# Output stage of a hybrid decoder layer: the subtractions that make the low parts of the feed-forward operands are queued behind the next tile's norm

## The chip, the cores and the metric

The kernel runs on one core of a Trainium2 chip. The core has TensorE (PE: products and transposes, results into PSUM), VectorE (DVE), ScalarE (ACT), GpSimd (POOL, which reads and writes SBUF here) and a queue, SyncE (SP), that issues all loads and stores. Each engine takes its own instructions in order; between engines there are semaphores. The metric is device time of one execution in microseconds, lower is better; several runs give a median.

## What is computed

One layer of a decoder with 1024 tokens, plus 16 meta tokens, and width 1024:

```python
u = rmsnorm(h, attn_norm_w[l]); proj = u @ w_in[l]
o_gdn = gated_deltanet_group(...)
o_fox = forgetting_attention_group(...)
h = h + concatenate([o_gdn, o_fox], -1) @ w_out[l]
x = rmsnorm(h, ffn_norm_w[l])
h = h + (silu(x @ w_gate) * (x @ w_up)) @ w_down
return rmsnorm(h, final_norm_w)[:, 16:]
```

The change touches what lies between the third last and the second last line of the layer: the residual sum after the output projection, the norm, and the preparation of `x` for the feed-forward products.

## The kernel before

All large products take operands that are split in two: a high part (ScalarE casts the value to the matmul type) and a low part (value minus high part), and three products high x high, high x low, low x high are summed. So every operand needs a cast on ScalarE and a subtraction on VectorE or GpSimd.

The output stage works on eight tiles of 128 tokens, in the order 0, 4, 1, 5, 2, 6, 3, 7 (`ORDER`). Tile t and tile t + 4 belong together: the feed-forward products follow a Strassen-like scheme with seven products p1 to p7 over 2 x 2 blocks, and the sums of its left operands are made from such a pair of tiles. For each tile the stage does this:

1. `prep_load`: a load of the attention output `of` (512 KB) is issued on SP; GpSimd sums its two halves (L1133); ScalarE spreads the softmax reciprocals `rinv` into the half that came free (L1134).
2. `prep_pe`: TensorE transposes that half (`rbt`, L1144), VectorE multiplies (L1145), ScalarE casts and VectorE subtracts (`split`, L161 and L162), which gives `ohl`.
3. `load_h` loads the residual `hst`, whose slot is that of the tile two before.
4. `out_fox(tt, 0)` and `out_fox(tt, 1)`: twelve products each (`wof`, `wx`) for the left and the right half of the columns; VectorE adds each to `hst` (L1177). In six of the tiles (4, 5, 2, 6, 3, 7) the second half has twelve further products ahead of it, `fox_g`, for the DeltaNet group.
5. `norm2`, behind the second half: ScalarE squares and sums (L1067), VectorE makes the mean (L206), GpSimd takes the power -1/2 (L207), VectorE scales (L1069); the result is `xn2`, in the trace `xn`. A store of `hst` follows.
6. `u_blocks`: TensorE transposes `xn2` into two PSUM banks (`u2t`, L1248; three banks take turns). In tiles 0 to 3 the inner function `put` makes p1 and p2, each a cast (L1253) and a low part (L1254, VectorE), and ScalarE copies both banks into `br` (L1261) for the partner tile. In tiles 4 to 7 VectorE forms the differences (L1267 to L1271, GpSimd one at L1273) and `put` makes p6, p3, p7 with VectorE and p5, p4 with GpSimd (`ul_p` are the low parts, `uh_p` the high ones).

`u_blocks` of a tile stands in the program between two halves of the next tile, so that its transposes run among the next tile's products: the transposes of tile 1, for instance, follow twelve products of tile 5. TensorE's order is the one of the program (`manual_schedule`). The orders of the other engines come from a scheduler that places each instruction by a timeline of its own when the program is built; `tc.issue_after(x)` adds that an instruction is placed behind x.

With tile 7 the first products of the feed-forward begin (`ga`, `ua`, then `gb`, L1343). Ahead of them VectorE and ScalarE split the weights (`wlo_g`, `wlo_u`, and from L1317 on the sums `ws`, `s4` and their splits); the latter stand behind tile 7's second residual sum (`last_h`).

## Time and profile before

| what | value |
|---|---|
| median of 3 runs | 1329.59 us (1329.17 to 1331.01) |
| profiled execution | 1326.59 us |
| its span | 1324.9 us |
| TensorE busy | 1294.3 us (98%) |
| VectorE, ScalarE, GpSimd busy | 853.2, 548.4, 440.6 us |
| output stage | about 605 to 700 us of the span |

The span is what the instructions cover; the execution has 1.7 us around it. The profiled execution is one run, 3.0 us below the median of the three. A row of an engine's timeline has the start, the duration, the line, what it writes and reads (numbers left out), and in brackets how long the engine had been idle and what ended that. A duration holds the instruction's start-up and its end, so rows that follow each other without a gap overlap by some 0.1 us (VectorE, ScalarE) or 0.15 us (TensorE).

### The profile page before, as it was taken

How to read it: one execution, taken by the hardware profiler on the slowest of the kernel's cores; microseconds unless marked ns; L12 is line 12 of the kernel's file. 1: busy time of each engine (PE TensorE's matmuls, PEld its weight loads, DVE VectorE, ACT ScalarE, POOL GpSimd, SP SyncE). 2: the span in 40 equal slices, each digit the busy share in tenths (PEclk: the TensorE clock that was granted, in tenths of full speed). 3: DMA queues.
4: the chain of work that ended last, by engine and by line, in shares of the span. 5: the costliest groups of instructions: out<-in, count | busy, mean ns of one | idle time of the engine just before them, and what ended most of it. 6: DMA issues, size and time to landing. Idle time of an engine off the chain costs nothing.

```text
span 1324.9 us, 20216 instructions
## 1 busy us (share of the span) xinstructions
PE 1294.3 (98%) x7442; PEld 1129.3 (85%) x7442; DVE 853.2 (64%) x1521; ACT 548.4 (41%) x918; POOL 440.6 (33%) x415
## 2 busy tenths in 40 slices
PE   8999999999999999999999999999999999999997
PEld 8999999899999877887777888888888888888886
DVE  6665889676236578896787665566666565355644
ACT  6543534232223477884553233333333343343332
POOL 2211323501022266661522644553334453010301
PEclk9999999999999999999999999999999999999999
DMA  6331743874479698746544555444444557945513
GB/s 227 98 112 33 212 133 116 221 209 143 150 246 329 195 271 233 206 114 199 182 144 130 188 183 183 147 140 159 159 162 156 175 193 271 400 176 189 210 62 128
DMA packets 192955, 237.93 MB, mean 180 GB/s; under 512 B 18896, under 2 KB 144712, under 8 KB 189144
## 3 DMA queue, kind: packets, MB, share of 16 engines
q1 hardware_dynamic: 192856, 236.65, 55.8%
q8 instruction: 58, 0.95, 0.3%
q14 instruction: 41, 0.34, 0.1%
HBM read 159.00 MB, written 77.60 MB: 179 GB/s over the span
## 4 chain that ended last, share of the span: by engine, by line
PE 76%; DVE 8%; DMA 7%; issue 3%; POOL 3%; ACT 1%; SPq 1%; POOLq 0%; DVEq 0%; ACTq 0%
PE xp L1506 8%; PE yp L1506 7%; PE gb L1343 5%; PE ud L1343 5%; PE ub L1343 5%; PE gd L1343 5%; PE ua L1343 4%; PE ga L1343 4%; PE pj_fk L201 4%; PE pj_fq L201 3%; PE ue L1343 2%; PE ge L1343 2%; PE pt L989 2%; PE fv L201 2%; DMA rkr<-rk_d 1%
## 5 line engine op out<-in xcount | busy, mean ns | idle before, releaser
L162 DVE TENSOR_TENSOR al_p<-ra_p,ah_p 128x2048 fp32r<-128x2048 f32 (+1 forms) x21 | 46.7, 2222 | 93.9 <-ACT ah_p L161 93.9
L942 POOL TENSOR_TENSOR bi<-ccol,cr 128x144 f32<-128x144 f32 (+7 forms) x60 | 70.6, 1182 | 50.8 <-DVE sm L958 35.6
L161 ACT CAST ah_p<-ra_p 128x2048 fp32r<-128x2048 f32 (+1 forms) x21 | 37.1, 1767 | 105.7 <-PE xp L1506 48.5
L1506 PE MATMUL xp<-wh_p,ah_p 128*128 128x512 f32 (+1 forms) x187 | 70.5, 377 | 0.7 <-DVE hs L1533 0.7
L1506 PE MATMUL xp<-wl_p,ah_p 128*128 128x512 f32 (+1 forms) x187 | 70.4, 377 | 0.0
L1506 PE MATMUL xp<-wh_p,al_p 128*128 128x512 f32 (+1 forms) x187 | 70.4, 376 | 0.0
L1396 POOL TENSOR_TENSOR gzw<-gzw,uzt 128x512 f32<-128x512 f32 x11 | 18.4, 1676 | 154.4 <-DVE uzt L1387 128.5
L1396 POOL TENSOR_TENSOR gxy<-gxy,uxy 128x512 f32<-128x512 f32 x22 | 38.9, 1769 | 66.6 <-DVE uxy L1387 57.4
L1343 PE MATMUL gb<-uh_p,w_g_p 128*128 128x512 f32 x176 | 57.8, 389 | 0.0
L1343 PE MATMUL gd<-uh_p,w_g_p 128*128 128x512 f32 x176 | 57.7, 389 | 0.0
L1343 PE MATMUL ud<-uh_p,w_u_p 128*128 128x512 f32 x176 | 57.7, 389 | 0.0
L1343 PE MATMUL ub<-uh_p,w_u_p 128*128 128x512 f32 x176 | 57.7, 389 | 0.0
L162 DVE TENSOR_TENSOR w_u_p<-raw_u,w_u_p 128x512 fp32r<-128x512 f32 x42 | 42.7, 1016 | 21.6 <-ACT w_u_p L161 21.5
L162 DVE TENSOR_TENSOR pl<-pt,ph 128x512 fp32r<-128x512 f32 (+1 forms) x96 | 51.8, 553 | 5.0 <-ACT ph L161 4.4
L161 ACT CAST ph<-pt 128x512 fp32r<-128x512 f32 (+1 forms) x96 | 45.2, 473 | 21.2 <-PE pt L989 20.5
L963 ACT ACTIVATE pr<-pr,sm 128x144 f32<-128x144 f32 (+3 forms) x64 | 50.6, 790 | 7.8 <-DVE sm L958 6.8
L1343 PE MATMUL ga<-uh_p,w_g_p 128*128 128x512 f32 x160 | 52.5, 389 | 0.0
L1343 PE MATMUL ua<-uh_p,w_u_p 128*128 128x512 f32 x160 | 52.5, 389 | 0.0
L1506 PE MATMUL yp<-wh_p,ah_p 128*128 128x512 f32 x132 | 51.3, 389 | 0.0
L1506 PE MATMUL yp<-wl_p,ah_p 128*128 128x512 f32 x132 | 51.3, 389 | 0.0
L1506 PE MATMUL yp<-wh_p,al_p 128*128 128x512 f32 x132 | 51.3, 389 | 0.0
L162 DVE TENSOR_TENSOR wl_p<-rw_p,wh_p 128x2048 fp32r<-128x2048 f32 (+1 forms) x21 | 46.9, 2235 | 3.4 <-ACT wh_p L161 3.4
(630 smaller groups left out, 4291.4 us busy)
## 6 DMA issues: line engine op xcount, KB each, us to landing
ra_p<-ao_p SPq DMA_DIRECT2D x14, 1024.0 KB, 4.7
raw_g<-in_w_gate_dram SPq DMA_DIRECT2D x22, 512.0 KB, 4.9
raw_u<-in_w_up_dram SPq DMA_DIRECT2D x22, 512.0 KB, 5.4
raw_d<-in_w_down_dram SPq DMA_DIRECT2D x22, 512.0 KB, 7.1
wt_p<-raw_d SPq DMA_DIRECT2D x33, 256.0 KB, 2.3
rw_p<-wt_p SPq DMA_DIRECT2D x8, 1024.0 KB, 5.7
kk<-k_d SPq DMA_DIRECT2D x14, 520.0 KB
rw_p<-in_w_down_dram SPq DMA_DIRECT2D x6, 1024.0 KB
```

Source lines behind the costliest of these rows:

```text
L161: cast = nc.scalar.copy(dst_hi, src)
L162: tail[0] = (cast, nc.vector.tensor_sub(dst_lo, src, dst_hi.bitcast(F32)))
L201: nc.tensor.matmul(dst, a, b, start=first, stop=last)
L942: nc.gpsimd.tensor_tensor(bi[:, :n], ccol[:, h, j:j + 1].broadcast_to([P, n]), cr[:, :n], op=ALU.subtract)
L963: nc.scalar.activation(pr[:, :n], pr[:, :n], AF.Exp, bias=sm[:, np_ - 1:np_], scale=-1.0, accum_out=rsum[:, h, j:j + 1])
L989: nc.tensor.transpose(pt[:rows_k, P * j:P * j + P], pts[j][0][:, c0:c0 + rows_k], ident)
L1343: nc.tensor.matmul(dst, a[:, c], b[:, k], start=(first and k == 0 and i == 0), stop=(k == 3 and i == 2), skip_group_check=not first)
L1396: last_mul[0] = G.tensor_tensor(gs[d], gs[d], us[d], op=ALU.mult)
L1506: nc.tensor.matmul(dst[:, n_], a[:, f, c], b[:, f, n_], start=(first and i == 0 and n == 0), stop=(i == NF - 1 and n == 2), skip_group_che ...
```

## The change

`norm2` returns its two last instructions, the power and the scaling. `put` no longer issues the low part, but keeps it in a list, `late`; the function `u_late` issues the list, each placed behind the power and the scaling of the tile whose norm was built last. `u_late` runs after the second half of the next tile. For the tiles 0, 4, 1, 5, 2 and 6 the low parts thus come behind the norm of 4, 1, 5, 2, 6 and 3. For the tiles 3 and 7 (`defer` false) the low part follows its cast as before. Casts, copies and differences are issued where they were.

```diff
--- before.py
+++ after.py
@@ -1065,8 +1065,8 @@
     def norm2(src, wb, dst, pool, nm):
         sst = pool.tile([P, 4], F32, tag="st2", bufs=2, name=f"st2_{nm}")
         nc.scalar.activation(dst, src, AF.Square, accum_out=sst[:, 0:1])
-        inv_rms(sst[:, 2:3], sst[:, 0:1], 1, 1.0 / D, sst[:, 1:2])
-        V.scalar_tensor_tensor(dst, src, sst[:, 2:3], wb, op0=ALU.mult, op1=ALU.mult)
+        pw = inv_rms(sst[:, 2:3], sst[:, 0:1], 1, 1.0 / D, sst[:, 1:2])
+        return pw, V.scalar_tensor_tensor(dst, src, sst[:, 2:3], wb, op0=ALU.mult, op1=ALU.mult)
 
     def wout_w(k0, nb):
         return w_out[P * k0:P * k0 + 256, 512 * nb:512 * nb + 512].rearrange("(k p) n -> p k n", p=P)
@@ -1156,7 +1156,7 @@
             nc.sync.dma_start(ht, h_d[tt])
         pre_u[tt] += (ht,)
 
-    accs, last_h = {}, [None]
+    accs, last_h, norms, late = {}, [None], [], []
 
     def fox_g(tt):
         if tt in fused:
@@ -1177,7 +1177,7 @@
         last_h[0] = V.tensor_add(hb, acc, hb)
         if nb:
             xn = wo_tile("xn2", [P, D], 2, tt)
-            norm2(ht, nwb2, xn, wo2, f"f{tt}")
+            norms[:] = norm2(ht, nwb2, xn, wo2, f"f{tt}")
             nc.sync.dma_start(h_d[tt], ht)
             xns[tt] = xn
 
@@ -1238,7 +1238,12 @@
         uo[p] = og["h"][i], og["l"][i]
     tops = {}
 
-    def u_blocks(tt):
+    def u_late():
+        with tc.issue_after(norms[0].ins), tc.issue_after(norms[1].ins):
+            while late:
+                late.pop(0)()
+
+    def u_blocks(tt, defer=True):
         xn, cols = xns[tt], slice(P * (tt % 4), P * (tt % 4) + P)
         pts = []
         for g in range(2):
@@ -1251,7 +1256,9 @@
         def put(p, src, eng=None):
             hi, lo = (t[:, :, cols] for t in uo[p])
             nc.scalar.copy(hi, src)
-            (eng or V).tensor_tensor(lo, src, hi.bitcast(F32), op=ALU.subtract)
+            late.append(lambda: (eng or V).tensor_tensor(lo, src, hi.bitcast(F32), op=ALU.subtract))
+            if not defer:
+                late.pop()()
 
         if tt < 4:
             br2 = wo_tile("br", [P, 2, 4, P], 1, tt, slot="br")
@@ -1429,10 +1436,11 @@
                     prep_load(ORDER[i + 2])
             if i > 2:
                 fox_g(tt)
-                u_blocks(ORDER[i - 1])
+                u_blocks(ORDER[i - 1], i < NT - 1)
             out_fox(tt, 1)
             if i < 3:
                 u_blocks(ORDER[i - 1])
+            u_late()
             if i == 2:
                 for m, v in (("g", w_g_v), ("u", w_u_v)):
                     raw0[m] = wraw.tile([P, WMAX], F32, tag="raw", name=f"raw_{m}")[:, :D]
@@ -1452,7 +1460,7 @@
         with tc.issue_after(last_h[0].ins):
             for m in "gu":
                 next(gens[m])
-        u_blocks(ORDER[7])
+        u_blocks(ORDER[7], False)
         for j in range(NF):
             ffn_in(j, () if j else done, None if j else gens)
             down_sums(j)
```

TensorE has the same instructions in the same order as before. VectorE, ScalarE, GpSimd and the load queue have the same instructions in another order. Three places follow, the second on two engines; a name such as `ohl_5_7713` is the tile `ohl` of token tile 5 and a buffer number.

ScalarE, tiles 0 and 4, from the cast of p1 to the square of tile 1's norm (`xn2_1`). Before:

```order
L1253 CAST uh_p1_7625<-u2t_0_0_7682 128x4x128
L1067 ACTIVATE xn2_4_7675,st2_f4_7676<-hst_4_7556 128x1024
L1253 CAST uh_p2_7629<-u2t_0_1_7687 128x4x128
L1261 COPY br_0_7692<-u2t_0_0_7682 128x512
L1261 COPY br_0_7692<-u2t_0_1_7687 128x512
L161 CAST ohl_5_7713<-of_5_7580 128x512
L1134 COPY of_2_7725<-rinv_96 128x512
L1067 ACTIVATE xn2_1_7743,st2_f1_7744<-hst_1_7660 128x1024
```

The same stretch of ScalarE's queue now:

```order
L1258 CAST uh_p1_7625<-u2t_0_0_7682 128x4x128
L1268 COPY br_0_7692<-u2t_0_0_7682 128x512
L1067 ACTIVATE xn2_4_7675,st2_f4_7676<-hst_4_7556 128x1024
L1258 CAST uh_p2_7629<-u2t_0_1_7687 128x4x128
L1268 COPY br_0_7692<-u2t_0_1_7687 128x512
L1134 COPY of_2_7725<-rinv_96 128x512
L161 CAST ohl_5_7713<-of_5_7580 128x512
L1067 ACTIVATE xn2_1_7743,st2_f1_7744<-hst_1_7660 128x1024
```

The first copy into `br_0` has moved ahead of the square of tile 4, and the spreading of `rinv` for tile 2 (`of_2`) ahead of the cast of tile 5's attention output (`ohl_5`).

ScalarE, tiles 4 and 1, from the last cast of tile 4 to the square of tile 5's norm. Before:

```order
L1253 CAST uh_p4_4146<-br_0_7692 128x4x128
L1134 COPY of_6_7807<-rinv_96 128x512
L161 CAST ohl_2_7795<-of_2_7725 128x512
L1442 ACT_TABLE_LOAD
L1442 ACTIVATE sil_7861<-mhalf_94 128x1
L1253 CAST uh_p1_7625<-u2t_1_0_7824 128x4x128
L1253 CAST uh_p2_7629<-u2t_1_1_7829 128x4x128
L1261 COPY br_1_7834<-u2t_1_0_7824 128x512
L1261 COPY br_1_7834<-u2t_1_1_7829 128x512
L1067 ACTIVATE xn2_5_7854,st2_f5_7855<-hst_5_7722 128x1024
```

The same stretch of ScalarE's queue now:

```order
L1258 CAST uh_p4_4146<-br_0_7692 128x4x128
L1134 COPY of_6_7807<-rinv_96 128x512
L1258 CAST uh_p1_7625<-u2t_1_0_7824 128x4x128
L1268 COPY br_1_7834<-u2t_1_0_7824 128x512
L1258 CAST uh_p2_7629<-u2t_1_1_7829 128x4x128
L1268 COPY br_1_7834<-u2t_1_1_7829 128x512
L161 CAST ohl_2_7795<-of_2_7725 128x512
L1450 ACT_TABLE_LOAD
L1450 ACTIVATE sil_7861<-mhalf_94 128x1
L1067 ACTIVATE xn2_5_7852,st2_f5_7853<-hst_5_7722 128x1024
```

The cast of tile 2's attention output (`ohl_2`) has moved behind the two casts and two copies that read tile 1's transposes, and each copy follows its cast.

GpSimd, tiles 4 to 2, from the power of tile 1's norm (`st2_f1`) to that of tile 2's. Before:

```order
L207 TENSOR_TENSOR st2_f1_7744<-st2_f1_7744,mhalf_94 128x1
L1133 TENSOR_TENSOR of_6_7807<-of_6_7807 128x512
L1254 TENSOR_TENSOR ul_p5_4147<-br_0_7692,uh_p5_4145 128x4x128
L1254 TENSOR_TENSOR ul_p4_4148<-br_0_7692,uh_p4_4146 128x4x128
L1133 TENSOR_TENSOR of_3_7889<-of_3_7889 128x512
L207 TENSOR_TENSOR st2_f5_7855<-st2_f5_7855,mhalf_94 128x1
L1273 TENSOR_TENSOR br_1_7834<-br_1_7834,ub_5_7916 128x512
L1254 TENSOR_TENSOR ul_p5_4147<-br_1_7834,uh_p5_4145 128x4x128
L1133 TENSOR_TENSOR of_7_7979<-of_7_7979 128x512
L1254 TENSOR_TENSOR ul_p4_4148<-br_1_7834,uh_p4_4146 128x4x128
L207 TENSOR_TENSOR st2_f2_7947<-st2_f2_7947,mhalf_94 128x1
```

The same stretch of GpSimd's queue now:

```order
L207 TENSOR_TENSOR st2_f1_7744<-st2_f1_7744,mhalf_94 128x1
L1259 TENSOR_TENSOR ul_p5_4147<-br_0_7692,uh_p5_4145 128x4x128
L1133 TENSOR_TENSOR of_6_7807<-of_6_7807 128x512
L1259 TENSOR_TENSOR ul_p4_4148<-br_0_7692,uh_p4_4146 128x4x128
L207 TENSOR_TENSOR st2_f5_7853<-st2_f5_7853,mhalf_94 128x1
L1133 TENSOR_TENSOR of_3_7889<-of_3_7889 128x512
L1280 TENSOR_TENSOR br_1_7834<-br_1_7834,ub_5_7916 128x512
L1133 TENSOR_TENSOR of_7_7979<-of_7_7979 128x512
L207 TENSOR_TENSOR st2_f2_7942<-st2_f2_7942,mhalf_94 128x1
L1259 TENSOR_TENSOR ul_p5_4147<-br_1_7834,uh_p5_4145 128x4x128
L1259 TENSOR_TENSOR ul_p4_4148<-br_1_7834,uh_p4_4146 128x4x128
```

A low part of tile 4 has moved ahead of tile 6's sum (`of_6`), and both low parts of tile 5 (the `ul` that read `br_1`) behind the power of tile 2's norm (`st2_f2`); tile 7's sum (`of_7`) still stands ahead of that power.

VectorE, tiles 6, 3 and 7, up to tile 7's second residual sum. Before, the low part p6 of tile 6 stood just ahead of the first row:

```order
L1177 TENSOR_TENSOR hst_3_7976<-wx_3_8059,hst_3_7976 128x512
L1254 TENSOR_TENSOR ul_p3_7634<-u2t_6_1_8077,uh_p3_7633 128x4x128
L1254 TENSOR_TENSOR ul_p7_7632<-ut_6_8083,uh_p7_7631 128x4x128
L206 TENSOR_SCALAR st2_f3_8113<-st2_f3_8113 128x1
L1177 TENSOR_TENSOR hst_7_8056<-wof_7_0_8119,hst_7_8056 128x512
L162 TENSOR_TENSOR wlo_g0_8184<-raw_g_7777,whi_g0_8183 128x512
L1069 SCALAR_TENSOR_TENSOR xn2_3_8112<-hst_3_7976,st2_f3_8113,nwb2_7451 128x1024
L162 TENSOR_TENSOR wlo_g0_8184<-raw_g_7777,whi_g0_8183 128x512
L162 TENSOR_TENSOR wlo_u0_8190<-raw_u_7779,whi_u0_8189 128x512 x2
L1254 TENSOR_TENSOR ul_p1_7626<-u2t_3_0_8146,uh_p1_7625 128x4x128
L1254 TENSOR_TENSOR ul_p2_7630<-u2t_3_1_8151,uh_p2_7629 128x4x128
L1177 TENSOR_TENSOR hst_7_8056<-wx_7_8133,hst_7_8056 128x512
```

VectorE's queue now, from the mean of tile 3's norm to the same sum:

```order
L206 TENSOR_SCALAR st2_f3_8108<-st2_f3_8108 128x1
L1177 TENSOR_TENSOR hst_7_8056<-wof_7_0_8119,hst_7_8056 128x512
L162 TENSOR_TENSOR wlo_g0_8184<-raw_g_7777,whi_g0_8183 128x512
L1069 SCALAR_TENSOR_TENSOR xn2_3_8107<-hst_3_7976,st2_f3_8108,nwb2_7451 128x1024
L1259 TENSOR_TENSOR ul_p6_7628<-ub_6_8082,uh_p6_7627 128x4x128
L1259 TENSOR_TENSOR ul_p3_7634<-u2t_6_1_8077,uh_p3_7633 128x4x128
L1259 TENSOR_TENSOR ul_p7_7632<-ut_6_8083,uh_p7_7631 128x4x128
L162 TENSOR_TENSOR wlo_g0_8184<-raw_g_7777,whi_g0_8183 128x512
L162 TENSOR_TENSOR wlo_u0_8190<-raw_u_7779,whi_u0_8189 128x512 x2
L1259 TENSOR_TENSOR ul_p1_7626<-u2t_3_0_8146,uh_p1_7625 128x4x128
L1259 TENSOR_TENSOR ul_p2_7630<-u2t_3_1_8151,uh_p2_7629 128x4x128
L1177 TENSOR_TENSOR hst_7_8056<-wx_7_8133,hst_7_8056 128x512
```

The three low parts of tile 6 (`ul_p6`, `ul_p3`, `ul_p7`) have moved behind the scaling of tile 3 (`xn2_3`), ahead of the weights' low parts and the low parts of tile 3. On VectorE the low part of `ohl_6` has moved in the same way behind the two first differences of tile 5, and in the load queue the load of `of_7` follows it.

## Rows read from the trace of the kernel before

**Rows 1.** The page, part 1, busy time of each engine in the whole span.

```profile
PE 1294.3 (98%) x7442; PEld 1129.3 (85%) x7442; DVE 853.2 (64%) x1521; ACT 548.4 (41%) x918; POOL 440.6 (33%) x415
```

**Rows 2.** TensorE's waits, from 605 to 706 us and then from 706 us to the end: who waited for whom, microseconds in total, times, the longest.

```profile
PE u2t L1248 <- DVE xn L1069: 3.2, 4, 1.6
...
PE gb L1343 <- DVE ul_p L1254: 0.8, 1, 0.8
...
PE xp L1506 <- DVE hs L1533: 0.7, 1, 0.7
```

**Rows 3.** TensorE's instructions in order of time around the transposes `u2t` of tiles 1, 5, 2 and 6 (start, duration, idle time before in brackets with what ended it).

```profile
640.01 0.40 PE L193 MATMUL wx<-whi_wo,ul_p 128*128 128x512 f32 x1
641.24 0.95 PE L1248 MATMUL u2t<-ident,xn 128*128 128x128 f32 x7 [0.83 <-DVE xn L1069]
...
650.67 0.40 PE L193 MATMUL wx<-whi_wo,ul_p 128*128 128x512 f32 x1
651.67 1.06 PE L1248 MATMUL u2t<-ident,xn 128*128 128x128 f32 x8 [0.60 <-DVE xn L1069]
...
661.10 0.40 PE L193 MATMUL wx<-whi_wo,ul_p 128*128 128x512 f32 x1
663.09 0.30 PE L1248 MATMUL u2t<-ident,xn 128*128 128x128 f32 x1 [1.60 <-DVE xn L1069]
...
672.51 0.40 PE L193 MATMUL wx<-whi_wo,ul_p 128*128 128x512 f32 x1
672.75 1.03 PE L1248 MATMUL u2t<-ident,xn 128*128 128x128 f32 x8
```

**Rows 4.** ScalarE's instructions in order of time: the casts `ohl` of tiles 4 and 5, the spreading of `rinv` for tile 2, and the two copies into `br_1`.

```profile
619.13 0.62 ACT L161 CAST ohl<-of 128x512 fp32r<-128x512 f32 x1 [3.44 <-DVE of L1145]
...
632.71 0.62 ACT L161 CAST ohl<-of 128x512 fp32r<-128x512 f32 x1 [1.81 <-DVE of L1145]
635.24 0.62 ACT L1134 COPY of<-rinv 128x512 f32<-128x512 f32 x1 [1.90 <-POOL of L1133]
...
646.20 1.13 ACT L1261 COPY br<-u2t 128x512 f32<-128x512 f32 x2 [0.33 <-DVE ul_p L1254]
```

**Rows 5.** GpSimd's instructions in order of time: the sum of tile 2, the sum of tile 6 and two low parts of tile 4, the sum of tile 7, a low part of tile 5 and the power of tile 2.

```profile
633.75 1.45 POOL L1133 TENSOR_TENSOR of<-of 128x512 f32<-128x512 f32 x1 [3.84 <-DMA of<-o_d]
...
640.03 2.19 POOL L1133 TENSOR_TENSOR of<-of 128x512 f32<-128x512 f32 x1 [2.04 <-ACT uh_p L1253]
642.19 3.44 POOL L1254 TENSOR_TENSOR ul_p<-br,uh_p 128x512 fp32r<-128x512 f32 x2
...
658.14 1.72 POOL L1133 TENSOR_TENSOR of<-of 128x512 f32<-128x512 f32 x1
659.83 1.29 POOL L1254 TENSOR_TENSOR ul_p<-br,uh_p 128x512 fp32r<-128x512 f32 x1
661.09 0.54 POOL L207 TENSOR_TENSOR st_f<-st_f,mhalf 128x1 f32<-128x1 f32 x1
```

**Rows 6.** The chain of waits, in order of time (start, duration, what): the loads of `of` for tiles 2 and 3.

```profile
627.80 5.79 DMA of<-o_d
...
644.62 3.61 DMA of<-o_d
```

**Rows 7.** TensorE's instructions in order of time: the first `wof` product and the `rbt` transposes after it, for tile 4 and for tile 5, and the first `wof` product of tile 2.

```profile
619.80 0.50 PE L191 MATMUL wof<-whi_wo,ohl 128*128 128x512 f32 x1 [0.65 <-ACT ohl L161]
...
622.93 0.60 PE L1144 MATMUL rbt<-ident,of 128*128 128x128 f32 x4
...
634.15 0.48 PE L191 MATMUL wof<-whi_wo,ohl 128*128 128x512 f32 x1
...
637.01 0.60 PE L1144 MATMUL rbt<-ident,of 128*128 128x128 f32 x4
...
644.91 0.39 PE L191 MATMUL wof<-whi_wo,ohl 128*128 128x512 f32 x1
```

**Rows 8.** Line 1254, the low parts: count, shortest, median and longest duration in ns, by engine and source.

```profile
L1254 DVE TENSOR_TENSOR ul_p<-u2t,uh_p x12: 673/680/692, 628.1 to 699.7; 128x512 fp32r<-128x512 f32 x12
L1254 POOL TENSOR_TENSOR ul_p<-br,uh_p x8: 1291/1740/1844, 642.2 to 699.4; 128x512 fp32r<-128x512 f32 x8
L1254 DVE TENSOR_TENSOR ul_p<-ub,uh_p x4: 681/1122/1670, 638.6 to 697.5; 128x512 fp32r<-128x512 f32 x4
```

**Rows 9.** The load queue (SP) in order of time: the issues of `of` for tiles 6 and 7.

```profile
634.20 0.32 SPq L1132 DMA_DIRECT2D of<-o_d  x1
...
653.64 0.32 SPq L1132 DMA_DIRECT2D of<-o_d  x1
```

**Rows 10.** VectorE's instructions in order of time: the scaling of tile 2; then tile 7's first residual sum, the low parts of tile 3, tile 7's second residual sum, and the low part behind which `gb` waits.

```profile
661.66 1.28 DVE L1069 SCALAR_TENSOR_TENSOR xn<-hst,st_f,nwb 128x1024 f32<-128x1024 f32 x1 [1.53 <-POOL st_f L207]
...
679.34 0.69 DVE L1177 TENSOR_TENSOR hst<-wof,hst 128x512 f32<-128x512 f32 x1 [0.32 <-PE wof L193]
...
683.56 1.28 DVE L1254 TENSOR_TENSOR ul_p<-u2t,uh_p 128x512 fp32r<-128x512 f32 x2
685.85 0.69 DVE L1177 TENSOR_TENSOR hst<-wx,hst 128x512 f32<-128x512 f32 x1 [1.01 <-PE wx L193]
...
697.51 1.67 DVE L1254 TENSOR_TENSOR ul_p<-ub,uh_p 128x512 fp32r<-128x512 f32 x1
```

## Prediction

> **What bounds the kernel now.** First the page: TensorE is busy in 98% of the span, so whatever moves the time has to move TensorE [rows 1]. Next TensorE's waits, from 605 us (the last attention products) to 706 us (the feed-forward products are running), and from there to the end [rows 2]. After 706 us nearly nothing waits, 0.7 us in 619. Between them TensorE waits for the scaled tile (`u2t` behind `xn`) 3.2 us in four waits, and 0.8 us for a low part at the first `gb`. A microsecond won or lost at the start of `gb` is thus a microsecond of the run. Third, the places [rows 3]: without a wait the transposes start 0.24 us after the product ahead of them (672.51 to 672.75). For tile 1 it takes 1.23, for tile 5 1.00, for tile 2 1.99: losses of 0.99, 0.76 and 1.75, 3.50 in all. That is everything the edit can win there, 0.26% of the run. The fourth wait, tile 7's 0.2 us, is not deferred work and stays.
>
> The sum is made against the profiled execution, 1326.59 us (span 1324.9); the median of the three runs is 1329.59, 3.00 more, and I carry the difference over to the median. About 0.2% of it, 2.7 us, is what a measurement can tell from no change.
>
> **The change, part by part.** No instruction is added or removed. What moves is the order, and not only the low parts: the scheduler places ScalarE, GpSimd and the load queue anew, while TensorE's order is the same, row for row.
>
> *1. ScalarE at tile 5's cast, a new wait.* Before, the cast of tile 5's attention output (`ohl_5`) starts at 632.71 and the spreading of `rinv` for tile 2 (`of_2`) follows at 635.24 [rows 4]. The spread had to wait for GpSimd's sum of tile 2 (633.75, 1.45 long [rows 5]), and this for a load issued at 627.80 that took 5.79 us [rows 6]. None of these three comes later or earlier by the change. In the new order the spread stands ahead of the cast. ScalarE runs its queue in order, so the cast starts where the spread ends, about 635.76. At 619 the same pair shows what follows: cast at 619.13, first product at 619.80, 0.67 later [rows 4, 7]. So TensorE's `wof` of tile 5 starts at 636.43, where it started at 634.15 without a wait: 2.28 lost. In that older case the twelve products up to `rbt` took 3.13 (619.80 to 622.93), since the low part comes behind the cast; undisturbed they took 2.86 (634.15 to 637.01): 0.27 more [rows 7]. Cost 2.55; nothing hides it, as TensorE's next rows all stand behind it.
>
> *2. The wait for tile 1 goes, but through that stall.* TensorE reaches tile 1's transposes at 642.8 (640.25 + 2.55). The scaling is ready then: its square, sum and power follow the cast on ScalarE, and it starts at about 639.7, as before. Gain 0.99. The deferral alone would have won it, too; it can be won only once.
>
> *3. ScalarE at tile 2's cast.* In the new order `ohl_2` stands behind the four reads of tile 1's transposes, and the first copy into `br_1` needs the `br_0` buffer that GpSimd's last low part of tile 4 reads. GpSimd has, from the power's end at about 639.65, a low part, tile 6's sum and a low part. With the rows of before (2.19 and 3.44 for these three [rows 5]) that is over at 645.3; with three of the shortest, 1.29 each [rows 8], at 643.5. Three copies and casts, some 1.6 together (two copies took 1.13 [rows 4]), then the cast, then 0.67: TensorE's `wof` of tile 2 could start between 645.8 and 647.6 and is due at 646.5 (644.91 [rows 7] + 2.55 - 0.99). Stall between 0 and 1.1, with 0.27 behind it; I take 0.7 in all, near the middle. This holds if tile 6's load lands by 641.4: it is issued behind the low part of `ohl_5`, at about 637.2 instead of 634.20 [rows 9], and gets 4.2 us; alone in the queue such a load took 3.61 [rows 6], beside others 5.79.
>
> *4. The wait for tile 5 goes* for the same reason as in 2: TensorE is late and the scaling is in time. Gain 0.76.
>
> *5. The wait for tile 2, the largest.* Before, GpSimd stands between square and scaling: low part, tile 7's sum (658.14, 1.72), low part (659.83, 1.29), then the power at 661.09, and VectorE waits for it 1.53 [rows 5, 10]. In the new order both low parts come behind the power, but tile 7's sum stays ahead of it, and its load is issued later: behind the low part of `ohl_6`, which two subtractions on VectorE now precede. It was issued at 653.64 [rows 9]; with TensorE 1.5 late (2.55 - 0.99 + 0.7 - 0.76) I get 656.05. Landing 3.61 later, sum 1.3, power 0.55, scaling 1.28: the transposes can start at 663.0, and are due at 661.34 + 1.5 = 662.8. Of the 1.75 all but about 0.2 to 0.4 goes; I take 0.3. A load of 4.5, the most that tile 7's can have taken before (653.64 to 658.14), makes it 1.1.
>
> At this point (2.55 - 0.99 + 0.7 - 0.76 - 1.75 + 0.3) TensorE stands where it stood before, within 0.1 us.
>
> *6. VectorE at the entry of the feed-forward.* Tile 3's scaling and tile 7's sum are not waited for by TensorE; behind them VectorE is the bound. From tile 7's first residual sum (679.34) it runs through the scaling and the weights' low parts to tile 3's low parts (683.56, 1.29 for two), ends at 684.77, idles 1.01, and makes tile 7's second sum at 685.85 [rows 10]. From there it has no gap worth naming to the low part at 697.51, behind which `gb` waits. The new order puts three low parts of tile 6 into that stretch, which before ran ahead of 679.34 in time not needed. At 0.60 each (1.29 - 0.69) they are 1.80: 684.77 + 1.80 = 686.57 against 685.85, so 0.72 late, once the cover of 1.01 (and the 0.07 of the start) is gone. Two of the three read two operands in SBUF, and stand now beside GpSimd's two low parts of the same tile, as both follow the scaling. Such a row took 0.68 to 1.67, with PSUM as source always 0.67 to 0.69 [rows 8]: 0 to 1.0 more; I take 0.4. Cost 1.12.
>
> On this overlap the Trainium skill speaks against the change: its page "SBUF — State Buffer", section "Who interferes with whom", says that a VectorE instruction with two SBUF inputs and a GpSimd instruction that reads SBUF exclude each other, the later being blocked until the earlier ends. The rows agree in kind (0.68 against up to 1.67). By that rule the price would be one whole GpSimd row, 1.29 in place of 0.4, and the forecast 0.9 higher.
>
> Elsewhere the reads of the transposes' banks end later (in tiles 4, 5 and 6 the second four transposes wait for a low part that now follows their own scaling): 0.6 us behind the scaling, while the first four take 0.5: nothing where TensorE is late already. The copies into `br` are no longer behind the low parts, which is what lets ScalarE's order shift; no price of its own.
>
> **Sum:** 2.55 - 0.99 + 0.7 - 0.76 - 1.75 + 0.3 + 0.72 + 0.4 = +1.17. On the profiled execution 1327.8, on the median 1330.8. With part 3 at 0, part 5 at 0.1 and part 6 at 0.72 it is -0.1; with 1.4, 1.1 and 1.7 in their places, +3.3.
>
> **Rivals.**
> *A, it does what it says.* Tile 2's load lands early enough that ScalarE's exchange is free: at 3.61 instead of 5.79 the spread is done at 633.6 and the stall is 0.1. Then -3.50 + 0.1 + 0.3 + 1.12 = -2.0: 1327.6. With no entry price either, -3.1. For it: the 3.61 row. Against it: the load comes out of a queue that the change doesn't touch ahead of this point, and 5.79 is what it took. Chance 0.12.
>
> *B, slower: the loads of tiles 6 and 7 are as slow as the early ones.* Both are issued later by the new order of VectorE, and GpSimd's sums stand ahead of what TensorE waits for. It decides from 4.2 us from issue to landing on. At 4.7, the middle of the two rows, part 3 becomes 1.25 and part 5 1.4: +2.8, 1332.4; at 5.79 in both it is +4.5. For it: half of such loads here had company in the queue. Against it: later issue gives the transfers ahead of them time to drain. Chance 0.16.
>
> **How the numbers follow.** Forecast (new stalls eat the gain, -0.1 to +2.6 us): 0.72. A 0.12, B 0.16. Faster by over 0.2% needs A with no price at the entry: 0.04. Slower by over 0.2%: most of B and the upper edge of the forecast, 0.15. Within: 0.81. The range takes the forecast's bounds, part of B above and of A below, and the spread of the runs: 1328.4 to 1332.8.
>
> **What would show it.** Right: a TensorE wait of 2 us or more for ScalarE's `ohl` near 634; no wait for `xn` at tiles 1 and 5, at most 0.4 for tile 2; tile 7's second sum without idle time ahead of it and `gb` waiting longer than 0.8. Wrong: no wait near 634 (A), a wait above 1 us at the `wof` of tile 2 or at tile 2's transposes (B), or the entry of the feed-forward as early as TensorE.

## The result, and the profile after

The changed kernel takes 1333.45 us (median of 10 runs, 1331.79 to 1336.57), the one before 1329.41 us in the same comparison (10 runs, 1326.46 to 1334.4): ratio 1.003, 95% interval 1.0018 to 1.0042. It is slower by 2.4 to 5.6 us, and above the range of the prediction.

The profiled execution of after has a span of 1331.6 us. It enters the stage 2.87 us later than that of before: tile 0's transposes start at 629.03, in before at 626.16. The change touches nothing ahead of that, and in the traces of the other kernels below these transposes start anywhere from 626.09 to 635.75. So everything is measured from there: **the stretch** is the time from the start of tile 0's transposes to the second gate product (`gb<-ul_p`). It is 73.08 us before (626.16 to 699.24) and 76.93 after (629.03 to 705.96). The difference, +3.85, is the measured loss; behind the stretch TensorE waits no more than it did [rows 2], and from the second gate product to its last product it takes 618.6 us in both. TensorE's rows at the ends of the stretch, in before and then the first one in after (its last stands further below):

```profile
626.16 1.03 PE L1248 MATMUL u2t<-ident,xn 128*128 128x128 f32 x8
...
699.24 0.51 PE L1343 MATMUL gb<-ul_p,w_g_p 128*128 128x512 f32 x1 [0.81 <-DVE ul_p L1254]
```

```profile
629.03 1.03 PE L1253 MATMUL u2t<-ident,xn 128*128 128x128 f32 x8
```

TensorE's waits of after, from 605 to 715 us (who waited for whom, microseconds in total, times, longest):

```profile
PE u2t L1253 <- DVE xn L1069: 4.0, 3, 1.8
PE wof L191 <- ACT ohl L161: 2.4, 3, 1.3
PE rbt L1144 <- ACT of L1134: 1.9, 2, 1.1
PE gb L1350 <- DVE ul_p L1259: 0.8, 1, 0.8
```

Against [rows 2]: the wait for the scaled tile was to go and has grown from 3.2 to 4.0, in three places instead of four. TensorE's rows at the places of [rows 3, 7] (start, duration, idle time before and what ended it): the first products of tiles 5 and 2, the transposes of tiles 1, 5, 2, 6, 3 and 7, the second gate product:

```profile
638.50 0.50 PE L191 MATMUL wof<-whi_wo,ohl 128*128 128x512 f32 x1 [1.26 <-ACT ohl L161]
...
644.90 0.27 PE L1253 MATMUL u2t<-ident,xn 128*128 128x128 f32 x1
...
649.35 0.50 PE L191 MATMUL wof<-whi_wo,ohl 128*128 128x512 f32 x1 [0.65 <-ACT ohl L161]
...
655.74 0.49 PE L1253 MATMUL u2t<-ident,xn 128*128 128x128 f32 x3
...
666.73 0.52 PE L1253 MATMUL u2t<-ident,xn 128*128 128x128 f32 x3 [1.19 <-DVE xn L1069]
...
676.40 0.81 PE L1253 MATMUL u2t<-ident,xn 128*128 128x128 f32 x6
...
687.48 0.74 PE L1253 MATMUL u2t<-ident,xn 128*128 128x128 f32 x5 [1.75 <-DVE xn L1069]
...
698.28 0.95 PE L1253 MATMUL u2t<-ident,xn 128*128 128x128 f32 x7 [1.10 <-DVE xn L1069]
...
705.96 0.50 PE L1350 MATMUL gb<-ul_p,w_g_p 128*128 128x512 f32 x1 [0.81 <-DVE ul_p L1259]
```

The waits at tiles 1 and 5 are gone and stand as waits for ScalarE at the products of tiles 5 and 2. Tile 2 still waits, tile 3 waits 1.75 us where it did not wait at all, tile 7 waits 1.10 instead of 0.22. Why, VectorE's rows show (tile 2's scaling; then from tile 7's first residual sum over tile 3's scaling and tile 6's three low parts to tile 7's second sum and scaling; compare [rows 10]):

```profile
664.27 2.31 DVE L1069 SCALAR_TENSOR_TENSOR xn<-hst,st_f,nwb 128x1024 f32<-128x1024 f32 x1 [0.65 <-POOL st_f L207]
...
682.99 0.69 DVE L1177 TENSOR_TENSOR hst<-wof,hst 128x512 f32<-128x512 f32 x1 [0.32 <-PE wof L193]
683.60 1.51 DVE L162 TENSOR_TENSOR wlo_g<-raw_g,whi_g 128x512 fp32r<-128x512 f32 x1
685.03 2.30 DVE L1069 SCALAR_TENSOR_TENSOR xn<-hst,st_f,nwb 128x1024 f32<-128x1024 f32 x1
687.25 0.68 DVE L1259 TENSOR_TENSOR ul_p<-ub,uh_p 128x512 fp32r<-128x512 f32 x1
687.86 0.68 DVE L1259 TENSOR_TENSOR ul_p<-u2t,uh_p 128x512 fp32r<-128x512 f32 x1
688.46 0.67 DVE L1259 TENSOR_TENSOR ul_p<-ut,uh_p 128x512 fp32r<-128x512 f32 x1
...
692.06 0.68 DVE L1177 TENSOR_TENSOR hst<-wx,hst 128x512 f32<-128x512 f32 x1
...
696.85 1.28 DVE L1069 SCALAR_TENSOR_TENSOR xn<-hst,st_f,nwb 128x1024 f32<-128x1024 f32 x1 [0.44 <-POOL st_f L207]
```

and beside them GpSimd's (powers and low parts at tiles 2 and 3, the power of tile 7; compare [rows 5]):

```profile
663.68 0.56 POOL L207 TENSOR_TENSOR st_f<-st_f,mhalf 128x1 f32<-128x1 f32 x1
664.19 3.52 POOL L1259 TENSOR_TENSOR ul_p<-br,uh_p 128x512 fp32r<-128x512 f32 x2
...
682.75 0.55 POOL L207 TENSOR_TENSOR st_f<-st_f,mhalf 128x1 f32<-128x1 f32 x1 [2.48 <-DVE st_f L206]
683.27 2.98 POOL L1259 TENSOR_TENSOR ul_p<-br,uh_p 128x512 fp32r<-128x512 f32 x2
694.68 2.13 POOL L207 TENSOR_TENSOR st_f<-st_f,mhalf 128x1 f32<-128x1 f32 x1 [8.44 <-DVE st_f L206]
```

The same place at tile 3 in before (VectorE: weights' low part and scaling; then TensorE's transposes, which wait for nothing):

```profile
679.95 0.68 DVE L162 TENSOR_TENSOR wlo_g<-raw_g,whi_g 128x512 fp32r<-128x512 f32 x1
680.56 1.27 DVE L1069 SCALAR_TENSOR_TENSOR xn<-hst,st_f,nwb 128x1024 f32<-128x1024 f32 x1
```

```profile
681.98 1.06 PE L1248 MATMUL u2t<-ident,xn 128*128 128x128 f32 x8
```

The scaling took 2.30 and 2.31 us instead of 1.27 and 1.28 [rows 10], and the weights' low part ahead of it 1.51 instead of 0.68. Tile 3's scaling had no slack: in before it ended 0.15 us ahead of the transposes (681.83 to 681.98), just as at tile 2, where TensorE did wait for it (662.94 to 663.09) [rows 3, 10]. GpSimd's two low parts start with the end of the power, which is also the moment at which the scaling may start. So the change put them beside the row for whose sake they were moved.

### The profile page after: what moved, and what is told of

Read it like the earlier page. It is cut to its first block, busy times and chain, and to the rows that moved or that the text cites. A ratio compares the mean times of both kernels' runs of the same rounds, so it can differ in the third digit from the quotient of the medians.

```text
span 1331.6 us, 20209 instructions
## 1 busy us (share of the span) xinstructions
PE 1300.1 (98%) x7442; PEld 1134.3 (85%) x7442; DVE 857.9 (64%) x1521; ACT 548.2 (41%) x918; POOL 441.9 (33%) x415
## 4 chain that ended last, share of the span: by engine, by line
PE 78%; DVE 10%; DMA 6%; issue 3%; POOL 2%; SPq 1%; ACT 1%; POOLq 0%; DVEq 0%; ACTq 0%
PE xp L1514 8%; PE yp L1514 7%; PE gb L1350 4%; PE ud L1350 4%; PE gd L1350 4%; PE ub L1350 4%; PE ua L1350 4%; PE ga L1350 4%; PE pj_fk L201 4%; PE pj_fq L201 3%; PE ue L1350 2%; PE ge L1350 2%; PE pt L989 2%; PE fv L201 2%; PE wog L201 1%
```

## The experiments

**Theory:** the loss comes from VectorE and GpSimd working side by side at tiles 2 and 3 (the rows above), and from tile 6's three VectorE low parts at the entry of the feed-forward. **Rivals:** ScalarE's exchanged orders at tiles 5 and 2, with the rest inherited; the moved VectorE rows as such; late loads. Each kernel's trace gives the stretch, cut in four by TensorE's starts. All but the last column in us:

| kernel | to tile 2's transposes | to tile 3's | to tile 7's | to `gb` | stretch | ratio to before, 95% interval |
|---|---|---|---|---|---|---|
| before | 36.93 | 18.89 | 9.57 | 7.69 | 73.08 | |
| after | 37.70 | 20.75 | 10.80 | 7.68 | 76.93 | 1.003, 1.0018 to 1.0042 |
| e1, tile 6 at once | 37.87 | 19.47 | 9.57 | 7.68 | 74.59 | 1.0009, 0.9998 to 1.002 |
| e2, VectorE's only | 36.75 | 18.89 | 10.80 | 7.68 | 74.12 | 1.002, 1.0009 to 1.003 |
| e3, GpSimd's only | 36.26 | 20.74 | 9.57 | 7.68 | 74.25 | 1.0006, 0.9993 to 1.0019 |
| e4, spread behind cast | 37.93 | 20.74 | 10.81 | 7.68 | 77.16 | 1.0036, 1.0022 to 1.0049 |
| e9, VectorE's but tile 6 | 36.92 | 19.49 | 9.57 | 7.68 | 73.66 | 1.0001, 0.9989 to 1.0013 |
| e10, tile 5's GpSimd ones | 36.01 | 18.89 | 9.56 | 7.68 | 72.14 | 1.0003, 0.9989 to 1.0018 |
| e11, GpSimd's, behind scaling | 35.62 | 18.88 | 9.58 | 7.67 | 71.75 | 0.9993, 0.9982 to 1.0005 |
| e12, tile 5's, behind scaling | 34.95 | 18.90 | 9.58 | 7.68 | 71.11 | 0.9989, 0.9976 to 1.0002 |
| e13, change, behind scaling | 36.37 | 18.92 | 12.54 | 7.67 | 75.50 | 1.0019, 1.0009 to 1.003 |

Each row is one trace. Three pairs of kernels below (e6 and e11, e7 and e13, e8 and e12) have the same order of instructions on every engine: within such a pair the second to fourth column repeat within 0.04 us, but the first differs by up to 1.32. Small differences in the first column say little.

First four that undo one part each. Their expectations count from tile 4's first output product, 6.36 us ahead of tile 0's transposes, so that 79.44 there is 73.08 here and 83.30 is 76.93.

**Tile 6's low parts at once**, the others deferred:

```diff
-                u_blocks(ORDER[i - 1], i < NT - 1)
+                u_blocks(ORDER[i - 1], i < NT - 2)
```

> The low parts of tile 6, the last ones deferred, are formed at once; tiles 4, 0, 1, 5, 2 stay deferred. Stage (first output product of tile 4 to second gate product): 79.44 us before, 83.30 after. Theory (the loss lies at the entry of the feed-forward): tile 3's scaling and the gate weights' low part are back near 1.28 and 0.68, tile 7's second sum has idle time ahead of it again, stage about 80.2, time about +0.8 us on before. Rival (ScalarE's exchanged casts are the loss, the entry only inherits it): stage stays near 83, time +3 us or more. Rival (GpSimd's late power of tile 7 alone): stage about 82.5.

Measured: tile 7's column is back at 9.57, tile 3's scaling at 1.28, and the stretch falls by 2.34 to 74.59; tile 7's second sum again has 1.01 us of idle time ahead of it. That is some 0.7 more than expected: 0.58 stays at tile 3, whose power ends later behind GpSimd's rows (0.99 long instead of 0.55), and 0.94 at the front. So 2.34 of the 3.85 us hang on these five low parts and not on ScalarE's order, which here is that of after up to the feed-forward.

**GpSimd's low parts at once, VectorE's deferred** (in `put`):

```diff
-            if not defer:
+            if not defer or eng:
                 late.pop()()
```

> GpSimd's low parts are formed at once, as before; only VectorE's are deferred. Theory (VectorE's rows on two SBUF operands take longer beside GpSimd's low parts, which the change puts right behind the power): the scalings of tiles 1, 2, 3 take about 1.28 instead of 2.30, the gate weights' low part 0.68 instead of 1.51; tile 6's three VectorE low parts still stand at the entry (+0.7 us), stage about 81, time +1 to +1.8 us on before. Rival (the moved VectorE low parts are the price, not the overlap): stage stays at 82.5 or above. Rival (GpSimd's low parts ahead of the power bring tile 2's wait of 1.99 us back whole): stage 82 with the wait at tile 2 and not at the entry.

**VectorE's low parts at once, GpSimd's deferred:**

```diff
-            if not defer:
+            if not defer or not eng:
                 late.pop()()
```

> Only GpSimd's low parts are deferred behind power and scaling; VectorE's stand where they stood before, and ScalarE's order is that of before (cast of tile 5 ahead of the spread). Theory (overlap): the scalings of tiles 1, 2 and 3 take about 2.30 as in after though no VectorE low part has moved; tile 2's wait shrinks from 1.99 by about 0.5 only, stage about 79.5 to 80.5, time 0 to +1 us on before. Rival (overlap is an effect of the moved VectorE rows): scalings at 1.28, tile 2's wait all but gone, stage about 77.7, time -1.7 us. Rival (ScalarE's order): no stall at the output product of tile 5 in either case; if the stage is at 79.4 or less, ScalarE's order was the cause of what is lost up to tile 2.

These two halves take the loss apart without a remainder at the entry. With VectorE's half the step to tile 3 is 18.89, as before, and the step to tile 7 10.80, as after. With GpSimd's half it is 20.74, as after, and 9.57, as before. So 1.85 us belong to GpSimd's rows behind the power and 1.23 to VectorE's moved rows. The rival by which only moved VectorE rows overlap falls, too: in GpSimd's half VectorE's queue is the old one, yet the scalings of tiles 2 and 3 take 2.30 (tile 1's 1.28, against the expectation; the stretch, 80.6 by its count, is just above the 80.5 that it allowed), and at tile 3 the rows are those of after (VectorE: weights' low part, tile 3's scaling, tile 7's second sum; then GpSimd: power and two low parts):

```profile
682.09 1.51 DVE L162 TENSOR_TENSOR wlo_g<-raw_g,whi_g 128x512 fp32r<-128x512 f32 x1
683.52 2.30 DVE L1069 SCALAR_TENSOR_TENSOR xn<-hst,st_f,nwb 128x1024 f32<-128x1024 f32 x1
...
689.83 0.69 DVE L1177 TENSOR_TENSOR hst<-wx,hst 128x512 f32<-128x512 f32 x1 [1.01 <-PE wx L193]
```

```profile
681.24 0.55 POOL L207 TENSOR_TENSOR st_f<-st_f,mhalf 128x1 f32<-128x1 f32 x1 [2.66 <-DVE st_f L206]
681.75 2.98 POOL L1259 TENSOR_TENSOR ul_p<-br,uh_p 128x512 fp32r<-128x512 f32 x2
```

In VectorE's half they are 0.68 and 1.28 (weights' low part, scaling, tile 7's second sum; then GpSimd's low parts, done before the scaling, and tile 7's power):

```profile
686.59 0.68 DVE L162 TENSOR_TENSOR wlo_g<-raw_g,whi_g 128x512 fp32r<-128x512 f32 x1
687.19 1.28 DVE L1069 SCALAR_TENSOR_TENSOR xn<-hst,st_f,nwb 128x1024 f32<-128x1024 f32 x1
...
693.19 0.68 DVE L1177 TENSOR_TENSOR hst<-wx,hst 128x512 f32<-128x512 f32 x1
```

```profile
683.22 2.58 POOL L1259 TENSOR_TENSOR ul_p<-br,uh_p 128x512 fp32r<-128x512 f32 x2
...
695.82 2.13 POOL L207 TENSOR_TENSOR st_f<-st_f,mhalf 128x1 f32<-128x1 f32 x1 [9.51 <-DVE st_f L206]
```

The 1.23 are two things: the second sum comes 0.70 us later, counted from tile 6's transposes (13.80 instead of 13.10), and the power of tile 7 takes 2.13 instead of 0.93, so that its scaling waits 0.44 us for it. In before that power is this row, and nobody waits for it:

```profile
688.49 0.93 POOL L207 TENSOR_TENSOR st_f<-st_f,mhalf 128x1 f32<-128x1 f32 x1 [8.04 <-DVE st_f L206]
```

What the expectation of VectorE's half got wrong: tile 1's scaling still took 2.31, since one GpSimd low part still follows that power, and the stretch came out 0.5 below what was expected. The time of the whole, +1.2 to +4.0 us, lies just above the +1.04 of the stretch, for which I have no cause.

**ScalarE's spread behind the cast again**, the change otherwise as it is:

```diff
-        nc.scalar.copy(of[:, 4:8].rearrange("p m (i c) -> p (m i) c", i=2),
-                       rinv[:, :, tt:tt + 1].broadcast_to([P, FH, DH]))
+        with tc.issue_after(tail[0][0].ins):
+            nc.scalar.copy(of[:, 4:8].rearrange("p m (i c) -> p (m i) c", i=2),
+                           rinv[:, :, tt:tt + 1].broadcast_to([P, FH, DH]))
```

> The change with one order more: ScalarE's spread of rinv for a later tile stands behind the cast of the attention output ahead of it. Theory (entry): TensorE's stalls at the output products of tiles 5 and 2 go (1.26 and 0.65 in after), part of the waits at tiles 1 and 5 for the scaling comes back, the entry's loss of about 3 us stays: stage 82 to 83, time +2.5 to +3.5 us on before. Rival (ScalarE's exchange is the whole cause): stage 79 to 80, time within 1 us of before.

TensorE's waits for `ohl` fall from 2.4 to 0.7 us, and nothing is won: the stretch is 77.16 (83.5 by the count of the expectation, which had 82 to 83), and the wait for the scaled tile comes back, 2.14 at tile 5, whose power stands on GpSimd behind tile 3's sum, now 1.8 us later than before. The rival falls: the loss stays without the exchange. The time, +2.9 to +6.5 us, agrees with the stretch; most of it lies above the +3.5 that the theory had allowed.

**GpSimd's rows behind the scaling.** If the overlap is the cause, the deferral must work when GpSimd starts one row later. For that GpSimd first copies one column of the scaled tile:

```diff
+            rd = G.tensor_copy(seen, xns[tt][:, 0:1])
+            with tc.issue_after(rd.ins):
+                while late:
+                    late.pop(0)()
```

with `seen` a new buffer of 4 bytes a partition. Once with GpSimd's half alone, once with the whole change, once with tile 5's two low parts alone (`defer` only for i = 4), and the last without the copy:

> As the run in which only GpSimd's low parts are deferred, but GpSimd first copies one column of the scaled tile, so that its low parts start when the scaling has ended, not when the power has. VectorE's queue is that of before. Stretch from tile 0's first transposes to the second gate product: 73.08 us before, 76.93 after, 74.25 with GpSimd's low parts behind the power. Theory (the overlap lengthens the scaling): scalings of tiles 2 and 3 take 1.28 us again, TensorE's wait at tile 3 (1.75) goes, the one at tile 2 shrinks by about 1; GpSimd's low parts of tile 6 now lie beside the weights' low parts on VectorE, which have 1.01 us of idle time behind them: 71.4 to 72.4 us, time -0.7 to -1.7 us on before. Rival (what costs is GpSimd's late low parts as such, for whoever reads them or waits for GpSimd behind them): no gain on 74.25.

> The change as it is, with the same copy of a column on GpSimd, so that all low parts, GpSimd's too, start behind the scaling. Theory: scalings at 1.28 us, tile 3's loss of 1.85 and some 0.9 at tile 2 gone; tile 6's GpSimd low parts now lie beside the deferred VectorE ones, of which two read two SBUF operands, so that tile 7's loss of 1.23 stays or grows by up to 1.7: 74.1 to 75.8 us against 76.93 after and 73.08 before, time +1 to +2.7 us on before. Rival (ScalarE's order): 76.5 or more.

> Of all low parts only GpSimd's two of tile 5 are deferred, behind the scaling of tile 2 (by the copied column); everything else as before. Tile 2 has the largest wait of before, 1.60 us, with GpSimd's low parts ahead of its power. Theory: the wait falls to 0.4 or less, nothing else moves: 71.6 to 71.9 us against 73.08, time -1.2 to -1.5 us on before. Rival (TensorE's next dependency is as late): 72.8 to 73.1, no change.

> The same two low parts of tile 5 alone, deferred behind tile 2's power only, so that they run beside its scaling. Theory (overlap): the scaling takes 2.30 us in place of 1.28 and eats about 1 us of the 1.3 to 1.5 that the earlier power wins: 72.6 to 72.9 us, time -0.2 to -0.5 us on before. Rival (no effect of the overlap on the scaling): 71.7 as with the copied column.

The stretches are 71.56, 75.55, 72.45 and, without the copy, 72.14. The first two lie where the theory had them. The other two do not (71.6 to 71.9 and 72.6 to 72.9 were expected), though the step that they test, from tile 5's transposes to tile 2's, is 10.16 and 10.91 us (11.42 before), near what the theory asks; they miss at tiles 1 and 5. In e8, the third, GpSimd's sum for tile 6 happened to start 0.21 us ahead of tile 1's scaling (640.55 and 640.76): the sum took 1.28 us, the scaling 2.15, and TensorE waited 1.41 for it. In before the scaling started 0.22 ahead of the sum (639.81 and 640.03), and it was the sum that took longer, 2.19 [rows 5], and the scaling 1.28. In both traces it is the row that starts second that takes longer.

The times of the first three missed widely: ratios 1.0088 (1.0071 to 1.0105), 1.0119 (1.0104 to 1.0133) and 1.008 (1.0067 to 1.0093), some 11 to 16 us slower than before. All four ran on another chip than e1 to e4, but before took 1329.46 us there and e10, the fourth, 1330.41, so it is not the chip. The loss lies in the feed-forward, where nothing had been touched: from the second gate product to TensorE's last it is 630.6 us in each of the three and 618.6 in e10. The second form therefore writes the column into a free element of the statistics tile, and adds no buffer:

```diff
-            rd = G.tensor_copy(seen, xns[tt][:, 0:1])
+            rd = G.tensor_copy(norms[2][:, 3:4], xns[tt][:, 0:1])
```

> GpSimd's low parts alone deferred, behind the scaling, as in the run before it with the copied column; only the copy now goes to a free column of the statistics tile, so that no buffer of 4 bytes a partition is added. Theory (the added buffer moved the buffers behind it and with them made every feed-forward product slower, 0.234 instead of 0.227 us apart): products 0.227 apart again, the 11 us are gone; stretch from tile 0's transposes to the second gate product 71.4 to 71.8 us against 73.08 before, time -1.2 to -1.8 us on before. Rival (the late GpSimd rows themselves slow the feed-forward down): stays 10 us above before.

> Only tile 5's two GpSimd low parts deferred, behind the scaling of tile 2, without the added buffer. Theory: feed-forward products 0.227 us apart, tile 2's wait 0.4 or less, from tile 5's transposes to tile 2's 10.0 to 10.2 us (11.42 before, 10.91 when they stand behind the power only), stretch 71.8 us, time -1.2 us on before. Rival: the won time is lost again at the next dependency, stretch 72.9.

> The change as it is, with GpSimd's low parts behind the scaling and no added buffer. Theory: of the 3.08 us that the change loses at the entry, the 1.85 at tile 3 go; the loss at tile 7 rises from 1.23 to 2.5 to 3, since GpSimd's low parts now lie beside VectorE's deferred ones and the weights' low parts; stretch 75.0 to 75.6 us against 76.93 after, time +2 to +2.5 us on before. Rival (ScalarE's order is the loss): 76.5 or more.

All three are 12 to 13 us faster for it. The stretches of e11 and e13 lie where they were expected, that of e12 (71.11) 0.7 below. GpSimd's half behind the scaling has scalings of 1.28 us throughout and a stretch of 71.75; against the run with the same half behind the power, 74.25, the one thing that moved is when GpSimd starts. At the same place of it (VectorE: weights' low part, tile 3's scaling, further weights' low parts, tile 7's second sum; then GpSimd):

```profile
681.87 0.68 DVE L162 TENSOR_TENSOR wlo_g<-raw_g,whi_g 128x512 fp32r<-128x512 f32 x1
682.47 1.28 DVE L1069 SCALAR_TENSOR_TENSOR xn<-hst,st_f,nwb 128x1024 f32<-128x1024 f32 x1
...
684.26 2.39 DVE L162 TENSOR_TENSOR wlo_u<-raw_u,whi_u 128x512 fp32r<-128x512 f32 x2
...
687.77 0.68 DVE L1177 TENSOR_TENSOR hst<-wx,hst 128x512 f32<-128x512 f32 x1
```

```profile
683.81 0.58 POOL L1245 COPY st_f<-xn 128x1 f32<-128x1 f32 x1 [2.24 <-DVE xn L1069]
684.35 3.45 POOL L1263 TENSOR_TENSOR ul_p<-br,uh_p 128x512 fp32r<-128x512 f32 x2
```

The overlap has moved to the weights' low parts (2.39 for two, 1.28 before), where the idle 1.01 us [rows 10] takes it up: the step to tile 7 stays 9.58. With the whole change that cover is used already, and the same shift wins 1.83 at tile 3 and loses 1.74 more at tile 7 (12.54), as expected.

Tile 2 alone, without and then with the copied column, all engines in order of time (VectorE's scaling, GpSimd's two low parts, TensorE's first transposes):

```profile
669.24 3.51 POOL L1259 TENSOR_TENSOR ul_p<-br,uh_p 128x512 fp32r<-128x512 f32 x2
669.30 2.31 DVE L1069 SCALAR_TENSOR_TENSOR xn<-hst,st_f,nwb 128x1024 f32<-128x1024 f32 x1
...
671.76 0.41 PE L1253 MATMUL u2t<-ident,xn 128*128 128x128 f32 x2 [1.09 <-DVE xn L1069]
```

```profile
661.11 1.28 DVE L1069 SCALAR_TENSOR_TENSOR xn<-hst,st_f,nwb 128x1024 f32<-128x1024 f32 x1 [0.88 <-POOL st_f L207]
...
662.54 1.06 PE L1257 MATMUL u2t<-ident,xn 128*128 128x128 f32 x8 [0.35 <-DVE xn L1069]
662.60 2.99 POOL L1263 TENSOR_TENSOR ul_p<-br,uh_p 128x512 fp32r<-128x512 f32 x2
```

From tile 5's transposes to tile 2's it is 10.91 and 10.17 us, 11.42 before. The rest of e12's gain, at tiles 1 and 5, was not touched by it: their waits fell from 0.83 and 0.60 to 0.40 and 0.32, and they differ as much between other runs.

**VectorE's low parts deferred, but for tile 6's** (both edits of e1 and e2):

> VectorE's low parts deferred but for tile 6's, GpSimd's all at once: no overlap with a scaling, nothing moved to the entry; ScalarE's new order with its stalls at the output products of tiles 5 and 2 stays. If the parts add up (tile 3's 1.85 from the overlap, tile 7's 1.23 from tile 6's VectorE low parts), only -0.18 up to tile 2 is left: stretch 72.9 us against 73.08, time -0.2 us on before. Rival (ScalarE's stalls cost on their own): 74 to 75.5, time +1 to +2.5 us.

36.92 up to tile 2, as before, although TensorE waits 2.3 us for `ohl`; the 0.60 at tile 3 is that of e1, and the parts don't add up to 72.9 by as much: 73.66 lies between theory and rival. Time 1.0001. Against before, ScalarE's order costs nothing on balance in this trace: what TensorE loses at the products it gets back at the transposes. That it is free is not shown: e13 and e7, which have it and VectorE's deferral, reach tile 2 0.75 and 1.03 us later than e11 and e6, which have neither.

The fastest versions are e11 and e12, 1328.48 and 1328.61 us: both lie well below the changed kernel, and below before by a little that the intervals, 0.9982 to 1.0005 and 0.9976 to 1.0002, do not settle.

## Why the prediction was wrong

Each step by TensorE's starts in after against before, counted from tile 0's transposes:

| step of the prediction | forecast | measured |
|---|---|---|
| 1, ScalarE at tile 5's cast | +2.55 | +1.79 |
| 2, tile 1's wait | -0.99 | -1.00 |
| 3, ScalarE at tile 2's cast | +0.7 | +1.17 |
| 4, tile 5's wait | -0.76 | -0.76 |
| 5, tile 2's wait | -1.45 | -0.43 |
| 6, entry of the feed-forward | +1.12 | +3.08 |
| sum | +1.17 | +3.85 |

**What was right.** Steps 2 and 4 to 0.01; they are waits of before that went whole. Step 1 in mechanism (in after ScalarE's spread starts at 637.31, the cast at 637.83, the products at 638.50), with a load that came 0.6 us earlier than the row taken over, so that the stall was 1.26 where a sign of being right asked for 2 or more; step 3 between its bounds. That the four cancel the gain was right, and e9 and e2 agree, without the overlap at tile 2: -0.01 and -0.18 up to there, where steps 1 to 5 had +0.05. In step 6 the 0.72 for the three low parts measured 0.70.

**What failed is the term for the overlap of VectorE and GpSimd in step 6: 0.4 with an upper end of 1.0.** The mechanism was named; its size and its places were wrong. Step 6 put the overlap among tile 6's low parts, "as both follow the scaling". VectorE's do, and none of them took longer (0.68, 0.68, 0.67). GpSimd's stand in GpSimd's own queue behind the power, and nothing holds them back until VectorE has scaled: at tile 3 they ran from 683.27 to 686.25, the scaling from 685.03 to 687.33. So they ran beside the scaling, which takes twice as long as a low part (1.28 us) and which TensorE waits for as soon as it is late: "not waited for by TensorE" was true of before, but without slack. It took 1.02 more at tile 3, with 0.83 in the weights' low part ahead of it: 1.85. At tile 2 it took 1.03 more, which is why step 5 fell short: with 1.28 in place of 2.31 the transposes at 666.73 would have come 1.03 earlier, 0.56 behind the product at 665.14 instead of 1.59, and the step would have been -1.46 against the -1.45 forecast. Less the 0.4 that the sum had for the overlap, the two are 2.48 of the gap of 2.68 (3.85 - 1.17); the rest is the power below, +0.53, and some -0.3 from steps 1 to 4. Two smaller readings of the prediction: the row that it has end at 684.77 ends at 684.84 (684.77 is where the next one could start), and the load's issue at 656.05 in step 5 has no working for 0.91 us of it; counted from tile 0's transposes it came 2.09 us later than in before, not 2.41.

The Trainium skill, "SBUF — State Buffer", section "Who interferes with whom", says that a VectorE instruction with two SBUF inputs and a GpSimd one that reads SBUF exclude each other. The rows agree in kind, and go further than I granted: VectorE lost 1.85 us beside two GpSimd rows of 1.29 each, and GpSimd 0.40 (2.98 instead of 2.58). Priced by that rule at one whole GpSimd row, as the prediction had it beside its sum, step 6 would still have come out 1.1 too low, since there are two such rows.

**Second and smaller:** tile 7's power took 2.13 instead of 0.93 us, and that made 0.53 of the 1.23 at tile 7. It takes 2.13 in every trace in which VectorE's low parts of tile 6 are deferred (after, e2, e4, e7, e13) and 0.93 in all others; e9 differs from e2 by these low parts alone. Why is open. VectorE's rows beside it don't explain it: in before and in after the same three on two SBUF operands run without a gap, the first 0.16 us ahead of the power. What does differ beside it is that ScalarE copies `gxy` ahead of a weight's cast instead of behind it; no run takes that apart.

**The rivals.** A was rightly rejected: the stall was 1.26 us, not 0.1. B, the slow load, did not occur: tile 7's attention output was issued at 658.60 and its sum began at 662.43, 3.83 us later, under the 4.2 from which B decides; for tile 6 it was 3.64 (639.32 to 642.96). That a wait above 1 us at tile 2 was listed as B's sign was too coarse, since the overlap gives the same sign. `gb` waits as long as before, 0.8, since the delay had already been paid at tile 7's transposes.

## What to carry to other kernels

When work is moved off an engine's queue to clear the way for a row, look at what runs beside that row afterwards, on the engines whose rows lengthen each other in the trace: here the cleared way was the scaling, and the moved rows ran beside it. Here a deferred row had to stand behind the end of the critical row, not behind the row that releases it, and one tiny read of the result was enough to hold it back. It pays where the moved rows then meet idle time (e11: 2.50 us of the stretch against e3); in e13, where none was left, 1.74 of the 1.83 won at tile 3 was lost again at tile 7. And price each row that two engines can contend for at what the slow rows of the trace show, at all places where the new order brings them together, before the bounds are set.

## What the hardware showed that was not expected

A new buffer of 4 bytes a partition made every feed-forward product slower. The window from 720 to 820 us with the buffer and without it, for the kernels that defer only tile 5's low parts, e8 and e12 (TensorE's busy time and count first, the granted clock after the engines):

```profile
720.00:820.00 100.00, 100.00 (x430) 80.34 (x429) 63.92 (x89) 31.08 (x53) 56.50 (x35) 1.00 0.49 163
```

```profile
720.00:820.00 100.00, 100.00 (x443) 82.81 (x442) 63.66 (x87) 32.83 (x56) 57.60 (x36) 1.00 0.52 170
```

At a granted clock of 1.00, the upper of its two levels, and without a wait, 430 products run in 100 us instead of 443, 3% fewer; a product's row takes 395 ns in the mean from 740 to 1100 us instead of 389. Over the feed-forward's 414 us up to 1120 that is 12 us, and e8 is 12.0 above e12. The two kernels have the same instructions in the same order on every engine but for where one column is copied to. What is left is the place of the buffers behind the added one. That this is the cause is argued by elimination and shown by no run, and which operand's place would matter was not tried.
